# Seven block products in place of eight: the second output projection of a two-layer trunk

## The chip, the core and the metric

The kernel runs on one core of a Trainium2 chip. Its time is the device time of one execution in microseconds (us). It is written in a language in which the program gives each engine its instructions by name, and a planner sets the order on each engine's queue from priorities (program order) and its own estimate of durations. The engines are TensorE (PE; its weight loads are the row PEld), VectorE (DVE), ScalarE (ACT), GpSimd (POOL) and SyncE (SP), which here only starts DMAs.

## The reference

The input is one sequence of 1024 tokens of width 1024. Layer 0 is a differential attention, layer 1 a latent attention (MLA); both end in an output projection and a gated residual, and a last RMSNorm closes the trunk. What matters here is the end of layer 1:

```python
o = _from_blocks(lax.map(block, (_to_blocks(q_nope), _to_blocks(q_pe))))
o = o.reshape(b, s, MLA_WIDTH) * jax.nn.silu(z)
return o @ w_out                      # (1024 x 1024) @ (1024 x 1024)
...
x = x + gate * y                      # gate: one value per column
return _rmsnorm(x, final_norm_g)
```

## The kernel before

**Numbers in two parts.** Each float32 matrix operand is split into a high part, rounded to the format float32r (an ACT copy), and a low part, the rest (a subtraction on POOL or DVE). `mm3` (L184) multiplies high by high, high by low and low by high: three matmuls (L185, L186, L187) for one block of 128 rows by 512 columns.

**The second attention** (`attn1`, L1711) goes head by head; a head is eight row tiles of 128 queries. A tile is scores (L1704), softmax, transposes (L383), casts to high and low (L385 on ACT, L386 on DVE) and the product with the values (`pv`). Between them `fill` puts steps of the next head's projections into TensorE's gaps (`stream1`); their weight strips are split by L230 (ACT) and L231 (POOL). After each tile `extra` runs; in heads 0 to 6 it takes one step of `gate_steps` (56 steps), which computes the residual gate of layer 1 on DVE and stores it to DRAM (`gateS[1]`).

A finished half head goes through `finish` (L879): its row factors make a round trip through DRAM (L408, L410), POOL scales the tile (L885), ACT and POOL split it (L890, L891), and both parts are stored to DRAM (`oS`, L892, L893). `in_turn` keeps a POOL operation in program order, `behind` puts an operation behind a named one; the planner may move the rest.

**The second output projection** (`out_proj`, L1126) runs two groups of four token tiles, each over two column halves. For each of these four parts, all eight heads' weight blocks are loaded (L1088) and split (L1104 on ACT, L1105 on POOL), and four PSUM banks take 8 heads x 4 tiles x 3 matmuls. Then `resid` multiplies a bank by the gate, which is broadcast over the partitions (`oy`, L1152, DVE), and adds it to the residual tile (L1153). `done1` (L1826) takes the sum of squares (L1829, ACT), multiplies the first column half by the final gain on POOL (L1836) and, after the second half, computes the inverse root in seven small DVE operations (`rsqrt8k`, L178 to L181), scales both halves (L1843 on DVE, L1850 on ACT) and stores them. Two tiles, one tile, and one tile in two column pieces make the last part (`LAST`).

The last head (7) has no fills. There `extra1` loads the first group's attention output and the first weight blocks, and `PRE1` places five preparing steps, each one head of two tiles of the projection. Head 7's second half does not go through DRAM: `tail1` scales it by a product with a matrix of ones (L904), after a few projection matmuls.

Of the kernel before, what the change touches and what calls it, by code (L numbers as in the profile page):

```python
# [21 lines left out]
P = 128  # L22
# [24 lines left out]
V1_AT = (3, 2)  # L47
OT1_AT = 5
NORM_AT = 4
PRE0 = (0, 0, 0, 0, 0, 0, 1, 1, 1, 2, 1)  # L50
PRE1 = (0,0,0,0,0,0,1,1,1,1,1)
OW0 = (3, 4)
OP0 = (6, 4)
OW1 = (2, 4)
OP1 = (12, 4)
LAST = [(((0, 1, 2, 3), 0, HF),), (((0, 1), 0, HF), ((2,), 0, HF), ((3,), 0, 256), ((3,), 256, HF))]
Z_LAST = 4
# [9 lines left out]
X_ACT0 = (0, 2)  # L67
X_CUT = 256
WARM = (8, 9)
SIN_AT = (4, 5, 7)  # L70
# [16 lines left out]
def trunk(ctx: ExitStack, tc: tile.TileContext, A, out):  # L87
# [48 lines left out]
    vS = [[dr.tile([4, 2, P, 2, 4, P], F32, name=f"vS{l}_{f}") for f in range(2)] for l in range(2)]  # L136
    oS = [dr.tile([NH, 2, 2, P, HF], F32, name=f"oS{l}") for l in range(2)]
    x1S = dr.tile([NT, P, D], F32, name="x1S")
# [44 lines left out]

    def mm3(psum, ah, al, bh, bl, first, last):  # L184
        PE.matmul(psum, ah, bh, start=first, stop=False)  # L185
        PE.matmul(psum, ah, bl, start=False, stop=False)  # L186
        mm3.last = PE.matmul(psum, al, bh, start=False, stop=last).ins  # L187

# [690 lines left out]
    def finish(o, y, l, h, half, dst, ap_, dgs):  # L879

        if dst is None:
            b, rb = bcast_rows(ap_, y, "osq", 4)

            def scale():
                in_turn(G.tensor_mul(t3(o), t3(o), rb))  # L885
                hooks.append(split)

            def split():
                with behind("S"):
                    S.copy(b.bitcast(F32R), o)  # L890
                in_turn(G.tensor_sub(o.bitcast(F32R), o, b))  # L891
                SP.dma_start(oS[l][h, half, 0], b)  # L892
                SP.dma_start(oS[l][h, half, 1], o)  # L893
# [6 lines left out]
        rb = bank("m", "rb")  # L900
# [4 lines left out]
        V.tensor_mul(o, o, rb)  # L905
        hi, lo = dst
        S.copy(hi, o)
        V.tensor_sub(lo, o, f32v(hi))
# [217 lines left out]
    def out_proj(OT, ow, W0, pre, wpool, xpool, nlate, nx, xsrc, tile_done, group_done):  # L1126
# [4 lines left out]
        for gi in range(2):  # L1131
# [5 lines left out]
            for f in range(2):  # L1137
# [7 lines left out]
                for h in range(NH):  # L1145
                    W.append(W0[h] if first and h < len(W0) else ow.load(f, h))
                last = gi == 1 and f == 1

                def resid(i, a=0, b=HF, acc=None):
                    y = wpool.tile([P, HF], F32, name="oy", tag="oy", bufs=2)  # L1150
                    cs = slice(f * HF + a, f * HF + b)
                    V.tensor_mul(y[:, a:b], (acc or accs[i])[:, a:b], ow.gb[:, cs])  # L1152
                    add = V.tensor_add(fulls[i][:, cs], fulls[i][:, cs], y[:, a:b])  # L1153
                    tile_done(gi * 4 + i, fulls[i], cs.start, cs.stop, add)

                if last:
                    for tiles, a, b in LAST[ow.l]:
                        part = None
                        if a:
                            part = bank("acc", "oaccb")  # L1160
                        for h in range(NH):
                            for i in tiles:
                                mm_o(part or accs[i], OT, W, h, gi, i, slice(a, b))
                            if h % 2 or len(tiles) == 4:
                                side.tick()
                        for i in tiles:
                            resid(i, a, b, part)
                else:
                    for h in range(NH):
                        for i in range(2 if first and h < pre.n else 0, 4):  # L1170
                            mm_o(accs[i], OT, W, h, gi, i)
                        side.tick()
                    for i in range(4):
                        resid(i)
            group_done(gi, fulls)
# [10 lines left out]
    def extra0(i):  # L1186
# [3 lines left out]
        if i == Z_LAST:  # L1190
# [12 lines left out]
            ow = OutW(0, pw, *OW0)  # L1203
            ot = [lambda h=h: load_ot(OT[h][0], [oS[0][h, 0, i] for i in range(2)]) for h in range(NH - 1)]
            todo.extend(pre_plan(ot, ow, OW0[0], W0))
# [27 lines left out]
    mk.clear()  # L1233
    load_ot(OT[NH - 1][0], [oS[0][NH - 1, 0, i] for i in range(2)])
    st2b.close()
# [16 lines left out]

    def done0(tt, full, a, b, add):
        if b < D:
            return
# [24 lines left out]

    ot = [lambda h=h: load_ot(OT[h][1], [oS[0][h, 1, i] for i in range(2)]) for h in range(NH - 1)]
    side.add(None, None, *ot[:3], tail0, *ot[3:])
# [327 lines left out]
    def gate_steps():  # L1610
# [12 lines left out]
        for j in range(KT):  # L1623
# [9 lines left out]
        SP.dma_start(gateS[1].rearrange("(p j) -> p j", p=P), gcol1)  # L1633

    gate1 = gate_steps()


# [129 lines left out]
    stv.close()  # L1767
    ap2 = pool(st5, "attn1b")
    for h in range(NH - 1):
# [4 lines left out]
    assert next(gate1, 0) == 0  # L1774
    stw.close()
    stC.close()
    stO = ExitStack()
    op = pool(stO, "OT1", side="right")

    OT1 = [[pair(op, f"o1a{h}"), pair(op, f"o1b{h}") if h == NH - 1 else None] for h in range(NH)]  # L1780
    o7 = [op.tile([P, HF], F32, name="o17"), op.tile([P, HF], F32, name="dg17")]
    pw = pool(stO, "pw1", side="right")
    ow = OutW(1, pw, *OW1)
    W0 = []
    pre1 = Pre(OT1, W0)
    ot = [lambda h=h: load_ot(OT1[h][0], [oS[1][h, 0, i] for i in range(2)]) for h in range(NH - 1)]
    todo = pre_plan(ot, ow, OW1[0], W0)

    def extra1(i):
        for _ in range(-(-len(todo) // max(1, 7 - i))):  # L1790
            todo.pop(0)()
        for _ in range(PRE1[i]):
            pre1.step()

    def late1(o_, zz, gz):
# [3 lines left out]
        def f():  # L1799
            V.reciprocal(zz, zz)  # L1800
            finish(o, zz, 1, NH - 1, 1, OT1[NH - 1][1], None, dgs)

        return f

    tail1 = attn1(NH - 1, lambda i: (0, 0, 0, 0), extra1, late1)
    mk.clear()
    load_ot(OT1[NH - 1][0], [oS[1][NH - 1, 0, i] for i in range(2)])
    st5.close()
# [3 lines left out]

    psum("ps6", accx=5, m=1)
    st6 = ExitStack()
    p6 = pool(st6, "p6")
    for h in range(NH - 1):
        OT1[h][1] = pair(p6, f"o1b{h}")
    side.add(None, None, tail1, *[None] * OT1_AT, *[lambda h=h: load_ot(OT1[h][1], [oS[1][h, 1, i] for i in range(2)]) for h in range(NH - 1)])
    fg = p6.tile([P, D], F32, name="fg")
# [3 lines left out]
    held = []  # L1823
    w_ = [p6.tile([P, 1], F32, name=f"tw{tt}") for tt in range(NT)]

    def done1(tt, full, a, b, add):  # L1826
        ss = sm.tile([P, 1], F32, name="tss")
        junk = p6.tile([P, HF], BF16, name="tjunk", tag="tjunk", bufs=1)
        S.activation(junk[:, : b - a], full[:, a:b], AF.Square, accum_out=ss)  # L1829
        if tt == NT - 1 and b == D:  # L1830
            with tc.issue_after(add.ins):
                held.pop()()
        w = w_[tt]
        if a == 0:
            V.tensor_scalar(w, ss, 1.0 / D, EPS, op0=ALU.mult, op1=ALU.add)
            G.tensor_mul(full[:, a:b], full[:, a:b], fg[:, a:b])  # L1836
        else:
            V.scalar_tensor_tensor(out=w, in0=ss, scalar=1.0 / D, in1=w, op0=ALU.mult, op1=ALU.add)
        if b == D:
            y = rsqrt8k(w)[:, 0:1]  # L1840

            def second():
                V.scalar_tensor_tensor(out=full[:, HF:], in0=full[:, HF:], scalar=y, in1=fg[:, HF:], op0=ALU.mult, op1=ALU.mult)  # L1843
                SP.dma_start(out[tt][:, HF:], full[:, HF:])

            if tt == NT - 2:
                held.append(second)
            else:
                second()
            S.mul(full[:, :HF], full[:, :HF], y)  # L1850
            SP.dma_start(out[tt][:, :HF], full[:, :HF])

    out_proj(OT1, ow, W0, pre1, p6, p6, *OP1, [x1S[tt] for tt in range(NT)], done1, lambda gi, fulls: None)
    st6.close()
# [81 lines left out]
```

## Time and profile before

| what | value |
|---|---|
| median of 3 runs | 1436.45 us (1434.03 to 1439.59) |
| the profiled execution | 1437.65 us, of which the span of instructions is 1435.9 us |
| granted TensorE clock, mean | 0.996 |
| DMA | 213.18 MB, mean 148 GB/s |
| weight blocks of both output projections (`wor`) | 64 loads of 256 KB |
| second attention, head 7 | about 1290 to 1344 us |
| second output projection | first preparing step at 1326, last matmul at 1427 |

In the profile a busy TensorE is not TensorE at its peak, because its matmuls overlap: a 128x512 matmul of the projection has a duration of some 390 ns while the next one starts much earlier. So distances between starts are read, not durations. For the other engines durations can be added up. "Idle before" names what an engine waited for last.

### The profile page before, as it was taken

To read this page: it belongs to the slowest core of one execution; us is meant where nothing else is said; L and a number is where in the kernel's file an instruction comes from. 1 tells how busy PE (TensorE), PEld (TensorE's weight loads), DVE (VectorE), ACT (ScalarE), POOL (GpSimd) and SP (SyncE) were. 2 spreads that over 40 slices of the span, in tenths; PEclk is the share of its full clock that TensorE was granted. 3 is DMA by queue.
4 is the path that set the end of the run, shared out by engine and by line. 5 is a ranking of instruction groups with operands and counts; after the bars stand their busy time and mean duration, and the time that the engine had idled before them with its cause. 6 is when DMAs were issued, how large, how long until landed. Compare 5 with 4: busy or idle time off the path is not lost. (4 is left out here: it accounts for less than half of the span.)

```text
span 1435.9 us, 20702 instructions
## 1 busy us (share of the span) xinstructions
PE 1398.5 (97%) x7426; PEld 1165.9 (81%) x7426; DVE 921.5 (64%) x1377; ACT 727.2 (51%) x1287; POOL 612.9 (43%) x485
## 2 busy tenths in 40 slices
PE   9999999999999999998999999999999999999997
PEld 6777788888888887887787877887888888888886
DVE  8655777777777767677345985545666555555356
ACT  5523465656565655566343442345454454545342
POOL 5425264646464655454552234531141331412572
PEclk9999999999999999999999999999999999999999
DMA  9776533334342324237653146398343433336563
GB/s 343 244 242 204 185 89 107 82 110 118 103 111 85 104 77 112 58 96 263 230 175 125 37 133 205 123 299 242 112 135 106 135 105 82 97 102 205 185 237 135
DMA packets 135385, 213.18 MB, mean 148 GB/s; under 512 B 19057, under 2 KB 56049, under 8 KB 135282
## 3 DMA queue, kind: packets, MB, share of 16 engines
q1 hardware_dynamic: 135282, 211.86, 47.8%
q8 instruction: 58, 0.95, 0.3%
q14 instruction: 45, 0.37, 0.1%
HBM read 137.40 MB, written 50.80 MB: 131 GB/s over the span
## 5 line engine op out<-in xcount | busy, mean ns | idle before, releaser
L385 ACT CAST pth<-tr 128x512 fp32r<-128x512 f32 x256 | 150.3, 587 | 284.9 <-PE tr L383 283.1
L400 DVE TENSOR_REDUCE nm<-s 128x1 f32<-128x1024 f32 x192 | 233.9, 1218 | 69.9 <-PE s L847 58.4
L386 DVE TENSOR_TENSOR ptl<-tr,pth 128x512 fp32r<-128x512 f32 x256 | 176.0, 688 | 140.3 <-ACT pth L385 140.0
L231 POOL TENSOR_TENSOR wl<-wraw,wh 128x512 fp32r<-128x512 f32 (+2 forms) x79 | 105.1, 1333 | 205.1 <-ACT wh L230 170.1
L402 ACT ACTIVATE e<-s,nm 128x1024 f32<-128x1024 f32 x128 | 143.6, 1122 | 30.8 <-DVE nm L400 28.4
L383 PE MATMUL tr<-ident,e 128*128 128x128 f32 x1024 | 155.0, 274 | 2.5 <-DVE ptl L386 2.4
L383 PEld LDWEIGHTS tr<-ident,e 128*128 128x128 f32 x1024 | 121.1, 140 | 43.6 <-DVE ptl L386 19.4
L185 PE MATMUL acc<-h0h,wh 128*128 128x512 f32 x360 | 150.1, 417 | 1.0 <-DVE v_hl L363 1.0
L185 PE MATMUL pv<-pth,vt 128*128 128x256 f32 x512 | 147.6, 288 | 0.9 <-DMA vt<-vS 0.9
L186 PE MATMUL pv<-ptl,vt 128*128 128x256 f32 x512 | 145.7, 284 | 0.0
L187 PE MATMUL pv<-pth,vt 128*128 128x256 f32 x512 | 144.7, 283 | 0.0
L187 PE MATMUL acc<-h0h,wl 128*128 128x512 f32 x360 | 143.2, 398 | 0.6 <-POOL wl L231 0.6
L186 PE MATMUL acc<-h0l,wh 128*128 128x512 f32 x360 | 142.0, 394 | 0.0
L1105 POOL TENSOR_TENSOR wol<-wor,woh 128x512 fp32r<-128x512 f32 x64 | 85.5, 1358 | 84.9 <-ACT woh L1104 84.3
L185 PEld LDWEIGHTS pv<-pth,vt 128*128 128x128 f32 x512 | 97.4, 190 | 4.3 <-issue 1.1
L186 PEld LDWEIGHTS pv<-ptl,vt 128*128 128x128 f32 x512 | 97.6, 191 | 2.7
L187 PEld LDWEIGHTS pv<-pth,vt 128*128 128x128 f32 x512 | 97.6, 191 | 0.0
L847 PE MATMUL s<-ks,qa 128*128 128x512 f32 x256 | 82.6, 404 | 6.1 <-DVE e L855 4.4
L327 POOL TENSOR_TENSOR rp_r<-rp_raw,cosT 128x512 f32<-128x512 f32 x38 | 50.0, 1316 | 85.6 <-ACT rp_raw L324 38.6
L332 POOL TENSOR_TENSOR rp_sw<-rp_sw,sinT 128x512 f32<-128x512 f32 x42 | 55.2, 1314 | 73.2 <-DMA rp_sw<-rp_raw 73.1
L855 DVE SCALAR_TENSOR_TENSOR e<-s,z,e 128x1024 f32<-128x1024 f32 x64 | 82.1, 1283 | 2.1
L187 PEld LDWEIGHTS acc<-h0h,wl 128*128 128x128 f32 x360 | 67.6, 188 | 16.3 <-POOL wl L231 1.0
(599 smaller groups left out, 3370.9 us busy)
## 6 DMA issues: line engine op xcount, KB each, us to landing
ada<-in_ada_ss SPq DMA_DIRECT2D x32, 512.0 KB, 5.6
wraw<-in_w_s SPq DMA_DIRECT2D x64, 256.0 KB, 2.9
vS<-v_hl SPq DMA_DIRECT2D x32, 512.0 KB, 5.9
vt<-vS SPq DMA_DIRECT2D x32, 512.0 KB, 3.9
wor<-in_w_out SPq DMA_DIRECT2D x64, 256.0 KB, 3.6
rp_sw<-rp_raw SPq DMA_DIRECT2D x168, 64.0 KB, 2.0
bc_s<-bc_d SPq DMA_DIRECT2D x34, 256.0 KB, 4.2
oS<-bc_s SPq DMA_DIRECT2D x30, 256.0 KB, 2.4
```

The costliest lines, as they stand in the source:

```text
L185: PE.matmul(psum, ah, bh, start=first, stop=False)
L186: PE.matmul(psum, ah, bl, start=False, stop=False)
L187: mm3.last = PE.matmul(psum, al, bh, start=False, stop=last).ins
L231: sub = (V if pair_of else G).tensor_sub(l_[:, :n], raw[:, :n], f32v(h_[:, :n]))
L383: PE.transpose(tr[:, j, :], p[:, kt * P : (kt + 1) * P], ident)
L385: mk["S"] = S.copy(pth[kh][:, :, dst], tr).ins
L386: mk["V"] = V.tensor_sub(ptl[kh][:, :, dst], tr, f32v(pth[kh][:, :, dst])).ins
L400: mk["V"] = V.reduce_max(nm, s_ps, axis=AX.X, negate=True).ins
L402: mk["S"] = S.activation(e, s_ps, AF.Exp, bias=nm, scale=1.0, accum_out=zs).ins
L847: PE.matmul(s_ps[:, kc * HF : (kc + 1) * HF], src[:, c, ql], KS[h][kc][:, c, :], start=fst, stop=not fst)
L855: combined.append(V.scalar_tensor_tensor(out=e0, in0=e1, scalar=z1[:, 0:1], in1=e0, op0=ALU.mult, op1=ALU.add).ins)
L1105: in_turn(G.tensor_sub(lo, raw, f32v(hi)))
```

## The change

The 1024 x 1024 product is cut into 2 x 2 blocks of 512: A11 and A12 are the heads 0 to 3 and 4 to 7 of the first 512 tokens, A21 and A22 those of the second 512; B11 to B22 are the blocks of the output weights, already multiplied by the gate. Seven products and sums (Winograd's form of Strassen's scheme, which the kernel also uses for its gate path) take the place of eight:

| n | left operand | right operand | goes to (token half, column half) |
|---|---|---|---|
| 0 | A11 | B11 | all four |
| 1 | A12 | B21 | first, first |
| 2 | A21 + A22 - A11 | B22 - B12 + B11 | the other three |
| 3 | A21 + A22 | B12 - B11 | both halves of the second columns |
| 4 | A12 minus the left operand of 2 | B22 | first, second |
| 5 | A11 - A21 | B22 - B12 | second, both |
| 6 | A22 | B21 minus the right operand of 2 | second, first |

- `gate_steps` goes on after the gate is stored: in 28 more of its steps (28 to 55, from head 3's second half) it loads the gate and, head by head of four, the four weight blocks, multiplies them by the gate and forms the seven right operands on POOL, and stores them to DRAM (`tS`).
- The attention's output is stored whole (`oF`), not split. `pair_steps` forms the left operands of 2 to 5 on POOL: pairs 0 and 1 (heads 0 and 4, 1 and 5) in head 6, stored to DRAM (`sS`); pair 2 in head 7, kept in SBUF; pair 3 is formed by DVE in `tail1`.
- Before each product its blocks are fetched, and split by `split_a` (ACT and DVE; ACT and POOL in head 7) and `split_w` (ACT and POOL). PSUM banks Y hold products 0 + 2 + 5 + 6, banks Z first product 1 and then 3 + 4. Each time a bank is right for a quarter of the output, one DVE add puts it on the residual.
- In products 0 to 2 the head is the outer loop, in 3 to 5 the token tile. Tokens 0 to 511 are finished after product 4, with the inverse root on POOL; tokens 512 to 1023 after product 6, whose tiles go as before (`LAST1`).
- `PRE1` places four preparing steps of product 0 instead of five. `out_proj` loses its case for the last part; layer 0's work is the same.

```diff
+    oF = dr.tile([NH, 2, P, HF], F32, name="oF")
+    tS = dr.tile([7, 4, P, HF], F32, name="tS")
+    sS = dr.tile([4, 2, P, HF], F32, name="sS")
...
             def split():
+                if l == 1:
+                    SP.dma_start(oF[h, half], o)
+                    return
...
         SP.dma_start(gateS[1].rearrange("(p j) -> p j", p=P), gcol1)
+        yield
+        gb = [ut("gb", True, F32) for _ in range(2)]
+        for f in range(2):
+            SP.dma_start(gb[f], gateS[1][None, f * HF : f * HF + HF].to_broadcast([P, HF]))
+        for h in range(4):
+            (b11, b12), (b21, b22) = b_ = [[ap3.tile([P, HF], F32, name="ob", tag="ob", bufs=nob) for _ in range(2)] for _ in range(2)]
+            for m in range(2):
+                for f in range(2):
+                    SP.dma_start(b_[m][f], A["w_out1"][f, 4 * m + h])
+            yield
+            for f in range(2):
+                for m in range(2):
+                    in_turn(G.tensor_mul(b_[m][f], b_[m][f], gb[f]))
+            yield
+            for n, t in ((0, b11), (1, b21), (4, b22)):
+                SP.dma_start(tS[n, h], t)
+            t2 = ap3.tile([P, HF], F32, name="ot2", tag="ob", bufs=nob)
+            in_turn(G.tensor_sub(b12, b12, b11))
+            in_turn(G.tensor_sub(t2, b22, b12))
+            yield
...
+        yield from pair_steps(0)
+        yield
+        yield from pair_steps(1)
+
+    def pair_steps(h):
...
+        for t, (hh, half) in zip(a, ((h, 0), (h + 4, 0), (h, 1), (h + 4, 1))):
+            SP.dma_start(t, oF[hh, half])
+        yield
+        in_turn(G.tensor_add(a22, a21, a22))
+        in_turn(G.tensor_sub(a21, a11, a21))
+        in_turn(G.tensor_sub(a11, a22, a11))
+        in_turn(G.tensor_sub(a12, a12, a11))
...
+        def put(self, raw, hi, lo, eng):
+            with behind("S"):
+                S.copy(hi, raw)
+            sub = eng.tensor_sub(lo, raw, f32v(hi))
...
+    def add_to(tt, acc, f, a=0, b=HF, piece=False):
+        full = xs_[tt]
+        cs = slice(f * HF + a, f * HF + b)
+        add = V.tensor_add(full[:, cs], full[:, cs], acc[:, a:b])
...
+    for h in range(4):
+        for i in range(4):
+            sv.mm(2, Y[i], h, i)
+        if h == 1:
+            sv.fetch(4)
+            load_x1(1, 1)
+    for i in range(4):
+        add_to(i, Y[i], 1)
+
+    Z = [bank("z", "oz") for _ in range(4)]
+    for n, first, rows, acc, f, piece in ((3, True, 4, Z, 1, False), (4, False, 0, Z, 1, True), (5, False, 4, Y, 1, True)):
+        sv.split(n + 1)
+        for i in range(4):
+            for h in range(4):
+                sv.mm(n, acc[i], h, i, start=first)
...
+            add_to(rows + i, acc[i], f, piece=piece)
+            if i == 1 and n < 5:
+                sv.fetch(n + 2)
...
+    for tiles, a, b in LAST1:
+        acc = {i: bank("z", "oyb") if a else Y[i] for i in tiles}
+        for h in range(4):
+            for i in tiles:
+                sv.mm(6, acc[i], h, i, slice(a, b), start=a > 0)
+        for i in tiles:
+            add_to(4 + i, acc[i], 0, a, b, piece=True)
```

More of the change, by code (lines that the diff above doesn't have):

```diff
@@ L68 @@
 X_CUT = 256
+PAIR_AT = 4
 WARM = (8, 9)
@@ L1146, in out_proj @@
                     W.append(W0[h] if first and h < len(W0) else ow.load(f, h))
-                last = gi == 1 and f == 1
-                def resid(i, a=0, b=HF, acc=None):
-                    y = wpool.tile([P, HF], F32, name="oy", tag="oy", bufs=2)
[L1151 to L1174, printed above, removed]
+                for h in range(NH):
+                    for i in range(2 if first and h < pre.n else 0, 4):
+                        mm_o(accs[i], OT, W, h, gi, i)
+                    side.tick()
+                for i in range(4):
+                    y = wpool.tile([P, HF], F32, name="oy", tag="oy", bufs=2)
+                    V.tensor_mul(y, accs[i], ow.gb[:, fs])
+                    V.tensor_add(fulls[i][:, fs], fulls[i][:, fs], y)
+                    if f:
+                        tile_done(gi * 4 + i, fulls[i])
             group_done(gi, fulls)
@@ new lines, in trunk, with step, home_w @@
+    class Pre7:
+        n = 0
+        def step(self):
+            if not self.n:
+                self.accs = [bank("acc", "oy") for _ in range(2)]
+            for i in range(2):
+                sv.mm(0, self.accs[i], self.n, i, start=True)
+            self.n += 1
+    pw = pool(stO, "pw1", side="right")
+    sv = Seven()
+    sv.raw = lambda: pw.tile([P, HF], F32, name="wor", tag="wor", bufs=4)
+    def home_w(n, h):
+        pl, tag, nb = (pw, "wo", 8) if h < 2 else (p6, "wp", 8) if n else (wst, "whl", 6)
+        return [pl.tile([P, HF], F32R, name="wo" + x_, tag=tag, bufs=nb) for x_ in "hl"]
@@ L1789, in extra1 @@
+    todo += [lambda h=h: sv.fetch_a(2, h) for h in range(2)]
     def extra1(i):
+        if PAIR_AT <= i < 8:
+            next(pair2, None)
         for _ in range(-(-len(todo) // max(1, 7 - i))):
```

216 lines of the change are left out of this document (171 added, 45 removed).

## The prediction

> **What bounds the kernel now.** I read the page's engine table first, then the stretches from the middle of the second attention to the end, then the waits of TensorE there, then the timeline of the last 22 us. The engine table:
>
> ```profile
> PE 1398.5 (97%) x7426; PEld 1165.9 (81%) x7426; DVE 921.5 (64%) x1377; ACT 727.2 (51%) x1287; POOL 612.9 (43%) x485
> ```
>
> The stretches (columns: stretch, length, then busy us and count of PE, PEld, DVE, ACT, POOL, the granted clock, DMA share, GB/s) are: heads 3 to 6 of the second attention, head 7, the projection up to the two last-but-one tiles, and the end.
>
> ```profile
> 1130.00:1290.00 160.00, 160.00 (x972) 137.49 (x971) 86.82 (x119) 82.41 (x151) 49.28 (x39) 1.00 0.34 96
> 1290.00:1344.00 54.00, 54.00 (x348) 47.25 (x347) 28.69 (x42) 29.53 (x53) 15.89 (x13) 1.00 0.55 173
> 1344.00:1416.00 72.00, 71.30 (x314) 57.97 (x314) 34.31 (x72) 26.01 (x53) 45.82 (x33) 1.00 0.66 230
> 1416.00:1435.90 19.90, 11.58 (x74) 10.31 (x72) 14.63 (x47) 6.09 (x14) 3.04 (x3) 0.85 0.28 106
> ```
>
> TensorE is filled without a hole from 1130 to 1416, at the full granted clock. Busy alone could deceive, since matmuls overlap; the waits of TensorE from 1344 to the end settle it. There are two entries in all:
>
> ```profile
> PE oacc L186 <- POOL wol L1105: 0.7, 1, 0.7
> PEld oacc L186 <- POOL wol L1105: 1.1, 1, 1.1
> ```
>
> So until 1416 matmuls taken away shorten the run, as long as nothing else becomes late. The pace of one matmul comes from the stretch that holds only projection matmuls (its columns are PE, PEld, DVE):
>
> ```profile
> 1348.96:1413.80 64.84, 64.84 (x281) 52.85 (x282) 8.20 (x12) 1.00 0.68 239
> ```
>
> 64.84 / 281 = **0.231 us** for one 128x512 matmul, start to start.
>
> The last 20 us are another case. The timeline (start, duration, engine, line), TensorE first, then VectorE:
>
> ```profile
> 1415.94 0.40 PE L187 MATMUL oacc<-woh,o1b7l 128*128 128x512 f32 x1
> ...
> 1421.48 0.40 PE L187 MATMUL oacc<-woh,o1b7l 128*128 128x512 f32 x1
> ...
> 1427.30 0.28 PE L187 MATMUL oaccb<-woh,o1b7l 128*128 128x256 f32 x1
> ```
>
> ```profile
> 1415.67 1.40 DVE L1152 TENSOR_TENSOR oy<-oacc,gb 128x512 f32<-128x512 f32 x2 [0.96 <-PE oacc L187]
> 1416.99 2.60 DVE L1153 TENSOR_TENSOR xfull<-xfull,oy 128x512 f32<-128x512 f32 x2
> ...
> 1423.66 0.68 DVE L1152 TENSOR_TENSOR oy<-oacc,gb 128x512 f32<-128x512 f32 x1
> 1424.38 0.69 DVE L1153 TENSOR_TENSOR xfull<-xfull,oy 128x512 f32<-128x512 f32 x1
> ...
> 1428.21 0.42 DVE L1152 TENSOR_TENSOR oy<-oaccb,gb 128x256 f32<-128x256 f32 x1
> 1428.66 0.42 DVE L1153 TENSOR_TENSOR xfull<-xfull,oy 128x256 f32<-128x256 f32 x1
> ```
>
> Tiles 4 and 5 of the last group are ready at 1415.7 to 1416.3. Tile 6 is ready near 1421.9, but VectorE takes it at 1423.66, 1.8 us late; the last piece is ready near 1427.6 and taken at 1428.21. From 1415.7 on VectorE sets the pace: 20.2 us to the end of the span.
>
> **The change, part by part.** All terms are against the profiled execution (1437.65 us, of which 1435.9 are its span). It stands 1.2 us above the median of 1436.45, so a difference is carried over to the median unchanged.
>
> *Matmuls.* Before there are 2 token groups x 2 column halves x 8 heads x 4 tiles x 3 = 384. After there are 7 products x 4 x 4 x 3 = 336. The 48 fewer would be 48 x 0.231 = 11.1 us if TensorE set the end. It does so only up to the point where tiles 4 and 5 of the last part are ready, and the change takes 24 from each side of that point: before it, 384 - 48 = 336 become 336 - 24 = 312. **First term: 24 x 0.231 = -5.5 us.** The wait for L1105 above need not come again: -0.5 (bounds 0 and -1.1).
>
> *The end.* After, one add from PSUM stands where L1152 and L1153 stood, because the gate is now in the weights. If VectorE keeps its order and its lag, the stretch from the two tiles to tile 6's turn was 8.0 us (1415.67 to 1423.66), holding 4.0 of L1152 and L1153; two adds from PSUM at 0.69 leave 5.4. From there to the last piece was 4.55; without its L1152 pieces (0.68 + 0.42) it is 3.45. From the last add to the end of the span 1435.9 - 1428.66 = 7.2. Together 16.1, so -4.1. If VectorE keeps up with TensorE, the last piece is ready 24 x 0.231 = 5.5 us after the two tiles (before it was 11.6), and the end is 5.5 + 0.1 + 7.2 = 12.8 later, so -7.4. Tile 6 and the last tile now come twice as fast, so VectorE's lag is likelier than not to stay: **second term -5.2 us** (bounds -4.1 and -7.4).
>
> *Feeding the products.* A product is 48 matmuls, 11.1 us. For each, four weight blocks and four activation blocks are split: eight ACT casts, four POOL subtractions, four DVE subtractions. From 1344 to the end the groups are:
>
> ```profile
> L1104 ACT CAST woh<-wor 128x512 fp32r<-128x512 f32 x24 | 14.7, 617 | 32.3 <-DMA wor<-in_w_out 22.8 <-PE oacc L186 5.1 <-PE oacc L187 2.3
> L1105 POOL TENSOR_TENSOR wol<-wor,woh 128x512 fp32r<-128x512 f32 x26 | 35.6, 1392 | 24.9 <-ACT woh L1104 24.3 <-DMA wor<-in_w_out 0.3
> L1836 POOL TENSOR_TENSOR xfull<-xfull,fg 128x512 f32<-128x512 f32 x8 | 11.9, 1520 | 0.0
> L1153 DVE TENSOR_TENSOR xfull<-xfull,oy 128x512 f32<-128x512 f32 x15 | 18.4, 1252 | 0.0
> L1152 DVE TENSOR_TENSOR oy<-oacc,gb 128x512 f32<-128x512 f32 x15 | 10.3, 688 | 24.3 <-PE oacc L187 24.3
> ```
>
> Per product: ACT 8 x 0.62 = 4.9; POOL 4 x 1.39 = 5.6; DVE 4 x 0.69 to 1.25 for the subtractions plus 4 x 0.69 for the adds = 5.5 to 7.8. All lie under 11.1. The tight place is products 4, 5 and 6: from product 3 on the row tile is the outer loop, so the previous product's weight blocks come free only at its end. The next but one can be split from there on and is due 11.1 us later; ACT then POOL need 0.6 + 5.6 = 6.2. That leaves 5 us for the L1836 products and the final scaling that share these engines. The gate path of this layer is the near relative: it runs seven products per pair of heads, with one weight split per 12 matmuls, the same rate. In its whole stretch (880 to 990) its products waited for a split only here:
>
> ```profile
> PEld zacc L187 <- POOL wl L231: 1.5, 2, 1.1
> PE zacc L187 <- POOL wl L231: 0.7, 1, 0.7
> ```
>
> Its three pairs are 21 splits, so TensorE's own wait is 0.03 us a split, and 24 splits here would make 0.8. I take **+0.5 us** (bounds 0 and +4, the L1836 products all ahead of the splits once: 11.7 + 0.6 against 11.1 in each of three products).
>
> VectorE with two SBUF operands slows beside POOL: the pair at 1416.99 above takes 1.3 each while POOL works on L1836, and 0.69 at 1424.38 when POOL rests; L1152 with one PSUM operand stays at 0.69. [...]
>
> *Weights made during the attention.* From step 28 of the gate steps (head 3, tile 4) to the end of head 6, POOL gets 32 + 8 operations more and loses seven L891; ACT loses seven casts (L890). SP gets 62 more DMAs (18 loads of weights and gate, 28 stores of products, 8 loads and 8 stores of sums; 256 KB each) and loses 7 stores (L892, L893 become one). The rows for 1130 to 1290:
>
> ```profile
> L891 POOL TENSOR_TENSOR o<-o,bc_s 128x512 fp32r<-128x512 f32 x7 | 9.0, 1291 | 25.3 <-ACT bc_s L890 25.3
> L231 POOL TENSOR_TENSOR wl<-wraw,wh 128x256 fp32r<-128x256 f32 x3 | 2.2, 736 | 16.7 <-ACT wh L230 16.7
> SPq L408 <- DVE zz L1723: 49.5, 7, 9.3
> SPq L1715 <- DVE o L1722: 16.4, 5, 10.5
> wraw<-in_w_kn SPq DMA_DIRECT2D x2, 128.0 KB, 2.3
> vt<-vS SPq DMA_DIRECT2D x6, 512.0 KB, 3.4
> ```
>
> POOL rises from 49.3 to 49.3 + 40 x 1.29 - 9.0 = 92 us of 160, DMA traffic from 96 GB/s by (62 - 7) x 0.26 MB / 160 us = 90 to 186 GB/s, about head 7's level, where TensorE did not wait either. What counts is order: POOL's operations here are kept in program order, so a burst of four multiplications (5.2 us) stands ahead of a strip's lower half (L231). The timeline of TensorE in head 5 shows the beat, two tiles from score to score and the fills (acc) between:
>
> ```profile
> 1212.45 0.39 PE L187 MATMUL acc<-ckh,wl 128*128 128x512 f32 x1
> ...
> 1216.08 0.63 PE L1704 MATMUL s<-kn_h,qn_h 128*128 128x512 f32 x2
> ...
> 1219.29 0.39 PE L187 MATMUL acc<-ckh,wl 128*128 128x512 f32 x1
> ...
> 1220.42 0.40 PE L187 MATMUL acc<-ckh,wl 128*128 128x512 f32 x1
> ...
> 1223.87 0.40 PE L187 MATMUL acc<-ckh,wl 128*128 128x512 f32 x1
> ...
> 1227.42 0.63 PE L1704 MATMUL s<-kn_h,qn_h 128*128 128x512 f32 x2
> ```
>
> Two tiles are 11.3 us, so a gate step is 5.7. A strip is needed two fill steps after its split; the fills come 6.8, 1.1 and 3.5 us apart, so two steps are 4.6 to 10.4 us, and after the cast and the subtraction about 3 us remain in the worst case. A full burst would then cost 5.2 - 3 = 2.2 us; with four weight bursts and two of sums the worst is 13 us, nothing at all is the other end. Most split points have the longer distance: I take **+1 us**.
>
> *Head 7.* POOL goes from 5 weight splits and one L891 to 17 operations (15.9 + 14 = 30 of 54 us), ACT from 5 casts to 13 (29.5 + 5 = 34.5 of 54). A cast put ahead of a transposed tile's cast delays TensorE by at most 0.62; 8 more would be 5 us, none 0. ACT mostly waits for TensorE there, so **+0.5 us**. One preparing step fewer (4, not 5) is only moved, and counted in the 336. The loads (18 blocks against 19) stay.
>
> Sum: -5.5 - 0.5 - 5.2 + 0.5 + 1 + 0.5 = **-9.2 us**: 1428.4 for the profiled execution, 1427.2 on the median, say **1427 us**.
>
> **The rivals.**
> - *The strips come late* (0.18). The POOL bursts hit half of the time at full price: +6.5 in place of +1, so -3.7: 1433. For it: strict order on POOL. Against: 68 us of room in 160.
> - *The splits come late at products 4 to 6* (0.10). POOL's 5.6 plus four L1836 (6.1) are 11.7 against 11.1, and ACT's final scaling is queued between; at most +4 in place of +0.5, so -5.7: 1431. Against: the gate path's 0.03 us a split.
> - *SP makes POOL stand* (0.14), the slower side. The weight loads of a round are issued one step (5.7 us) before POOL needs them and land 3 us after issue. SP already stands for up to 9.3 and 10.5 us behind one semaphore (rows above). If such a wait lies ahead of the loads, POOL stands for 9.3 + 3 - 5.7 = 6.6 us with the strip behind it, which costs 6.6 - 3 = 3.6 us, and the later blocks of the round follow. Over six rounds that is 22 us: 1427 - 1 + 22 = 1448. It decides once SP is more than 5.7 us late; below that it costs nothing. Against: a load that waits for nothing can be issued ahead of a waiting one when the order is planned.
> - That the matmuls do not become fewer cannot be: 336 follows from the loops.
>
> **How the numbers follow.** The forecast has 0.58: its own range is 1422 (all good ends: -5.5 - 1.1 - 7.4 = -14) to 1431. The late strips at 1433 and late splits at 1431 lie inside a range of **1422 to 1436**, which leaves out the slower rival (0.14) and some 0.03 of the strips' worst end (+13: 1439). About 0.5% (7.2 us, so 1429.3) is what a measurement of this kernel can tell from no change: faster is the forecast's 0.58 and half of the late splits, 0.63; same is the strips and the other half, 0.23; slower 0.14.
>
> **What would show it.** Right: TensorE still free of waits between products; about 67.5 us from the attention's last matmul to the point where the last part's first two tiles are ready (72 before, with 18 more matmuls in it); 13 to 16 us from there to the end; heads 3 to 6 as long as before. Wrong: TensorE waiting for POOL's strips in heads 4 to 6, PEld waiting for a weight block at the start of products 4 to 6, POOL idle with a DMA as the releaser during the weight rounds, or ACT casts ahead of the transposed tiles in head 7.

## The result: no difference, and the profile after

| what | before | after |
|---|---|---|
| median | 1439.51 us (22 runs, 1434.03 to 1445.95) | 1439.81 us (22 runs, 1432.23 to 1444.01) |
| ratio after / before | | 1.000, 95% interval 0.9987 to 1.0013 |
| profiled execution, its span | 1437.65, 1435.9 us | 1440.16, 1438.4 us |

The forecast was 1427 us, with 1422 to 1436 as its range. It was wrong: seven products take as long as eight. The engine table of the profile after, then its stretches (heads 3 to 6 of the second attention, head 7, the products up to the last part's first two tiles, the end; columns as in the prediction):

```profile
PE 1391.9 (97%) x7366; PEld 1159.4 (81%) x7366; DVE 934.3 (65%) x1368; ACT 729.8 (51%) x1295; POOL 660.2 (46%) x526
```

```profile
1132.30:1292.30 160.00, 160.00 (x972) 137.50 (x971) 87.41 (x119) 78.92 (x144) 91.66 (x72) 1.00 0.57 179
1292.30:1349.20 56.90, 54.12 (x341) 46.94 (x340) 30.61 (x45) 33.33 (x61) 24.60 (x19) 0.97 0.46 134
1349.20:1423.80 74.60, 69.59 (x298) 55.49 (x297) 50.79 (x65) 31.68 (x65) 53.06 (x40) 0.98 0.56 194
1423.80:1438.40 14.60, 6.21 (x39) 5.42 (x37) 10.26 (x42) 5.86 (x14) 0.00 (x0) 0.88 0.37 144
```

TensorE is busy for 7 us less, yet it now has holes in head 7 (54.12 of 56.90) and between the products (69.59 of 74.60), and in both the granted clock falls below 1.00. VectorE rises from 34.3 to 50.8 us in the third stretch. What TensorE waited for from 1350 to the end (us in all, times, longest) was VectorE's add L1969, never a weight block:

```profile
PE oy L186 <- DVE x L1969: 3.8, 2, 3.2
PE oz L186 <- DVE x L1969: 1.2, 2, 0.6
```

To compare parts, I measure between the same operations in both traces: VectorE's gating of a half head (L1722 before, L1760 after), the start of the attention's last pv matmul, the add for tile 4 in the last part (before: L1152), the end of the span.

| from, to | before | after | difference | prediction |
|---|---|---|---|---|
| the first half of head 0, the first half of head 7 | 1008.19 to 1323.79 = 315.6 | 1010.48 to 1326.26 = 315.8 | +0.2 | +1 |
| the first half of head 7, last pv | to 1343.70 = 19.9 | to 1349.17 = 22.9 | +3.0 | -0.9 |
| last pv, tile 4 of the last part | to 1415.67 = 72.0 | to 1423.76 = 74.6 | +2.6 | -4.2 |
| tile 4, the end | to 1435.9 = 20.2 | to 1438.4 = 14.6 | -5.6 | -5.2 |

In the prediction's column, 6 of the 24 matmuls fewer (the preparing step, 1.4 us) fall on head 7 and 18 (4.2 us) on the products. The four differences add up to +0.2. The other 2.3 us of the spans' difference arise before the first row, where every engine's instructions are the same; the variants below, which have these same instructions there, made that half of head 0 between 1004.7 and 1011.6 us, so it is chance between executions. Two parts came as predicted, and two lost what the others gained.

**Head 7.** ACT's timeline (start, duration, and in brackets the idle time before and its end):

```profile
1331.96 0.59 ACT L386 CAST pth<-tr 128x512 fp32r<-128x512 f32 x1
1336.07 0.62 ACT L1858 CAST oah<-wor 128x512 fp32r<-128x512 f32 x1 [3.52 <-DMA wor<-sS]
1336.60 1.11 ACT L403 ACTIVATE e<-s,nm 128x1024 f32<-128x1024 f32 x1
...
1337.70 0.57 ACT L386 CAST pth<-tr 128x512 fp32r<-128x512 f32 x1
1340.17 0.62 ACT L1858 CAST oah<-wor 128x512 fp32r<-128x512 f32 x1 [1.90 <-DMA wor<-sS]
```

The casts of product 2's left operands are written down after the attention, but the planner put them into ACT's queue ahead of the last softmax (L403) and of the transposed tiles' casts. In this trace ACT takes its queue in order: the softmax's input (nm, L401 on VectorE) was ready at 1332.7, but it stood behind a cast whose load SP had issued only at 1333.29. TensorE saw this two operations on, at the transposes, which wait for VectorE's L387:

```profile
1336.20 0.40 PE L188 MATMUL oy<-woh,oal 128*128 128x512 f32 x1
1339.38 1.11 PE L384 MATMUL tr<-ident,e 128*128 128x128 f32 x4 [2.78 <-DVE ptl L387]
...
1341.14 0.63 PE L188 MATMUL oy<-woh,oal 128*128 128x512 f32 x1
1341.57 0.63 PE L186 MATMUL oy<-woh,oah 128*128 128x512 f32 x1
```

After the pause the matmuls start 0.43 us apart instead of 0.23; the granted clock from 1339.38 to 1342.75 is 0.52. This slow clock did not make the head longer. In four variants below whose head 7 has the same casts in the same place (finish_later, splits_behind_adds, twelve_slots, weight_lows_by_act) TensorE kept its full rate, 0.23 us from start to start, paused twice, for 2.9 to 3.0 and 1.1 to 1.3 us, and the second row of the table is 22.8 to 23.1 us, as here. The casts' waits set the length.

**The products.** VectorE's timeline from the end of product 3 (products are numbered 0 to 6):

```profile
1388.72 1.27 DVE L1969 TENSOR_TENSOR x<-x,oz 128x512 f32<-128x512 f32 x2
1393.32 0.69 DVE L1859 TENSOR_TENSOR oal<-wor,oah 128x512 fp32r<-128x512 f32 x1 [3.33 <-ACT oah L1858]
...
1399.88 0.68 DVE L1969 TENSOR_TENSOR x<-x,oz 128x512 f32<-128x512 f32 x1
1401.40 0.16 DVE L1985 SCALAR_TENSOR_TENSOR tw<-tss,tw 128x1 f32<-128x1 f32 x1 [0.85 <-ACT tjunk L1975]
1402.58 0.75 DVE L1991 SCALAR_TENSOR_TENSOR x<-x,rq_y,fg 128x512 f32<-128x512 f32 x1 [1.02 <-POOL rq_y L2003]
1403.25 0.68 DVE L1969 TENSOR_TENSOR x<-x,oz 128x512 f32<-128x512 f32 x1
...
1415.41 0.68 DVE L1969 TENSOR_TENSOR x<-x,oy 128x512 f32<-128x512 f32 x1
```

At 1390.0 it reaches product 6's splits, which are queued ahead of product 3's last two adds, and stands for ACT, which stands for a load:

```profile
1392.67 0.62 ACT L1858 CAST oah<-wor 128x512 fp32r<-128x512 f32 x1 [9.01 <-DMA wor<-oF]
```

So product 4's first add comes at 1399.88, while TensorE had filled that bank by 1392.4 (the last of its 12 matmuls starts at 1392.15): a lag of 7.5 us. From there each tile of product 4 is finished in a chain: add, wait 0.85 for ACT's square, L1985, wait 1.0 for POOL's root, L1991. That is 1403.25 - 1399.88 = 3.4 us for each of the first two tiles, where TensorE makes one in 2.8 (12 x 0.231), so the lag isn't made up. The last two take 4.7 and 4.1 us; beside POOL's subtractions (1409.50 to 1413.73) L1991 takes 1.77 us in place of 0.75. Product 5's first add is done at 1416.1, and product 6 accumulates on the same banks:

```profile
1412.60 0.40 PE L188 MATMUL oy<-woh,oal 128*128 128x512 f32 x1
1416.24 0.47 PE L186 MATMUL oy<-woh,oah 128*128 128x512 f32 x1 [3.24 <-DVE x L1969]
...
1419.19 0.63 PE L186 MATMUL oy<-woh,oah 128*128 128x512 f32 x1
```

It can be worked out: from 1392.4 to product 6's turn at 1412.8 are 20.4 us; VectorE needs 1416.1 - 1399.9 = 16.2 from its first add. It may lag 4.2 us for nothing; it lagged 7.5, and TensorE waited 3.2. (The weight load's own entry for this wait, 3.7 us on PEld, names ACT's L1998, which was done at 1415.5; the load starts at 1416.20, right behind VectorE's add.)

### The profile page after: what moved, and what is told of

The parts are those of the page before. It is cut to its first block, busy times and chain, and to the rows that moved or that the text cites. A ratio compares the mean times of both kernels' runs of the same rounds, so it can differ in the third digit from the quotient of the medians.

```text
span 1438.4 us, 20700 instructions
## 1 busy us (share of the span) xinstructions
PE 1391.9 (97%) x7366; PEld 1159.4 (81%) x7366; DVE 934.3 (65%) x1368; ACT 729.8 (51%) x1295; POOL 660.2 (46%) x526
## 5 line engine op out<-in xcount | busy, mean ns | idle before, releaser
L401 DVE TENSOR_REDUCE nm<-s 128x1 f32<-128x1024 f32 x192 | 234.0, 1219 | 70.7 <-PE s L848 58.9
L387 DVE TENSOR_TENSOR ptl<-tr,pth 128x512 fp32r<-128x512 f32 x256 | 176.1, 688 | 136.5 <-ACT pth L386 136.0
L403 ACT ACTIVATE e<-s,nm 128x1024 f32<-128x1024 f32 x128 | 143.5, 1121 | 29.9 <-DVE nm L401 27.7
L328 POOL TENSOR_TENSOR rp_r<-rp_raw,cosT 128x512 f32<-128x512 f32 x38 | 49.9, 1314 | 90.1 <-ACT rp_raw L325 37.9
L848 PE MATMUL s<-ks,qb 128*128 128x512 f32 x256 | 80.6, 396 | 0.0
```

Of the source, the lines that this page charges most:

```text
L387: mk["V"] = V.tensor_sub(ptl[kh][:, :, dst], tr, f32v(pth[kh][:, :, dst])).ins
L401: mk["V"] = V.reduce_max(nm, s_ps, axis=AX.X, negate=True).ins
L403: mk["S"] = S.activation(e, s_ps, AF.Exp, bias=nm, scale=1.0, accum_out=zs).ins
L848: PE.matmul(s_ps[:, kc * HF : (kc + 1) * HF], src[:, c, ql], KS[h][kc][:, c, :], start=fst, stop=not fst)
```

## The experiments

Ratios are to the kernel before, run anew beside each group of variants; "us less" is what the ratio makes of that kernel's median (1437.7 to 1438.1 us), with an interval of some 2 to 3 us on either side. Lines below an edit can shift by some 10. "Distances" are the table's second and third rows, 22.9 and 74.6 us in the changed kernel.

**casts_behind**

```diff
-    mk.clear()
+    last_pth = mk.pop("S"); mk.clear()
...
-    sv.split(2)
+    with tc.issue_after(last_pth): sv.split(2)
```

> The ACT casts of product 2's left operands (L1858, oah<-wor) are put behind the attention's last cast of a transposed tile; nothing else moves. Measured by the distance from the store of head 7's first half (L891) to the attention's last pv matmul: 19.9 us before the change (1323.8 to 1343.7), 22.9 after it (1326.3 to 1349.2). Theory (ACT stands for the DMA of wor in front of exp and pth, and TensorE's clock drops after the pause): distance 19.5 to 20.5, TensorE's 2.8 us wait for DVE gone, time 3 to 4 us under the changed kernel, ratio to the kernel before 0.997 to 0.998. Rival 1 (the softmax shows because one preparing step is missing at tile 6): distance 22 to 23, ratio 1.000. Rival 2 (the head ends earlier, but the products then wait for their loads): distance near 20, ratio 1.000, a new DMA wait at products 0 to 2.

(The times named there, 1323.8 and 1326.3, are those of VectorE's gating of the half, not of its store.) Measured: 1433.2 us, ratio 0.9971 (0.9957 to 0.9984), 4.2 us less. Distances 19.2 (1323.72 to 1342.90) and 73.4. TensorE's longest wait in the head's last tiles, and the softmax on ACT:

```profile
1334.61 0.66 PE L384 MATMUL tr<-ident,e 128*128 128x128 f32 x4 [0.57 <-DVE ptl L387]
```

```profile
1330.27 1.11 ACT L403 ACTIVATE e<-s,nm 128x1024 f32<-128x1024 f32 x1 [0.26 <-DVE nm L401]
```

The theory holds: the wait of 2.8 is 0.57, and the products still had their own 3.2 us wait. The edit holds back all of product 2's splits; by the two traces what it moved out of the head's last tiles are three ACT casts and the three VectorE subtractions (L1859) that read them.

**step_at_tile_6**

```diff
-PRE1 = (0, 0, 0, 0, 0, 0, 0, 1, 1, 1, 1)
+PRE1 = (0, 0, 0, 0, 0, 0, 1, 1, 1, 1, 0)
```

> PRE1 gets a preparing step at tile 6 again and none at the last place (four steps as in the changed kernel); the casts stay ahead in ACT's queue. The distance from the store of head 7's first half to the last pv matmul now holds one step of 1.4 us more behind which work can hide. Theory (ACT stands for DMA): the casts still stand, 3.5 and 1.9 us, the step fills at most 1.4 us of TensorE's pause: ratio 0.999. Rival (missing step): the pause goes, ratio 0.997.

Measured: 1439.87 us, ratio 1.0011 (0.9996 to 1.0025). Distances 24.7 and 74.9. (Both kernels have the same four steps, 24 matmuls, ahead of the last pv; the step is only earlier.) The casts still stood, one of them longer:

```profile
1330.54 0.62 ACT L1858 CAST oah<-wor 128x512 fp32r<-128x512 f32 x1 [4.22 <-DMA wor<-sS]
```

TensorE's pause grew to 4.2 us, and the head took 1.8 us longer; the theory's own 0.999 lies outside the interval too. The rival is out: a step at tile 6 does not help while a cast waits for a load at the head of the queue.

**finish_later**

```diff
+        later.append([])
+        with tc.issue_after(add.ins):
+            for fn in later.pop(0):
+                fn()
...
-            V.scalar_tensor_tensor(out=w, in0=ss, scalar=1.0 / D, in1=w, op0=ALU.mult, op1=ALU.add)
...
+            later[0].append(root)
+            later[1].append(scale)
```

Here `root` makes tw and the root, and comes behind the next add; `scale` makes L1991 and the stores, behind the one after.

> The finishing of product 4's tiles is put off on VectorE: a tile's tw comes behind the next tile's add, its scaling (L1991) behind the one after; product 5's tw likewise. Same operations, other order. Theory (VectorE stands for ACT's square, 0.85 us, and POOL's root, 1.0 us, in each tile, so product 5's adds, which product 6 needs, come late): TensorE's waits for L1969 at product 6 (3.2 and 0.6 us) and the slow clock behind them (1.4 us) go, time 4 to 5.5 us under the changed kernel, ratio 0.996 to 0.997. Rival (VectorE is late by its amount of work, slowed beside POOL, and not by standing): the waits shrink by 1 us at most, ratio 0.999 to 1.000.

Measured: 1432.9 us, ratio 0.9957 (0.9937 to 0.9976), 6.2 us less; second distance 68.0. TensorE's waits from 1345 on are a single one, at product 4:

```profile
PE oz L186 <- DVE x L1969: 0.9, 1, 0.9
```

VectorE did the same work, still stood for the late loads (product 4's first add lags 6.4 us, at 1394.84), and the waits at product 6 were gone. So the chain is a necessary part of the loss.

**all_three**: the two edits and a third, which puts product 6's splits behind product 3's last add.

```diff
-        sv.split(n + 1)
+        with tc.issue_after(add3[-1]) if n == 5 else nullcontext(): sv.split(n + 1)
...
+            add3 = add3 + [add_to.last] if n == 3 else add3
```

> The casts behind, the finishing put off, and product 6's splits behind product 3's last add on ACT and VectorE (they stood 9.0 us for wor<-oF ahead of two adds). Theory: the losses are apart in time and add up, -3.5 - 5 - 1 to 1.5: time 1429 to 1431 where the kernel before has 1439.5, ratio 0.993 to 0.995. Rival (one loss only hides another: TensorE, no longer late, waits for the loads or splits of products 5 and 6): ratio 0.997 or more, with PEld waiting for L1858 or L1859.

Measured: 1428.03 us where the kernel before had 1437.66, ratio **0.9926** (0.9905 to 0.9948): 10.6 us less, the best of the study. The last two stretches and TensorE's only wait from 1335 to the end:

```profile
1340.30:1408.00 67.70, 67.03 (x297) 54.63 (x296) 50.53 (x64) 30.65 (x65) 50.64 (x39) 1.00 0.62 214
1408.00:1423.00 15.00, 6.28 (x39) 5.43 (x38) 10.71 (x43) 6.51 (x16) 2.04 (x2) 0.81 0.36 140
```

```profile
PE oz L186 <- DVE x L1969: 0.7, 1, 0.7
```

The gains add up within their intervals (4.2 + 6.2 = 10.4), and the distances, 67.7 and 15.0 us, are those of the prediction: about 67.5 and 13 to 16 us. The third edit shows no gain of its own that these intervals could tell.

**splits_behind_adds**: the changed kernel with only product 6's left splits moved, behind product 4's last add.

```diff
-                self.split_a(n, h)
+                with tc.issue_after(after) if after else nullcontext(): self.split_a(n, h)
...
-        sv.split(n + 1)
+        sv.split(n + 1, add_to.last if n == 5 else None)
```

> Product 6's splits of its left operands (ACT casts and L1859 on VectorE, which stood for wor<-oF until 1393 to 1397 ahead of product 3's last two adds and all of product 4's) are put behind product 4's last add. The finishing of a tile stays as it is: add, wait for ACT's square, tw, wait for POOL's root, L1991, 3.4 us per tile. Theory (the late loads start the lag, and the chain of 3.4 us against TensorE's 2.8 only keeps it): product 4's first add comes at once, near 3 us after the product's start and not 10, product 5's adds are done before product 6, TensorE's waits of 3.2 and 0.6 us go: ratio 0.996 to 0.997. Rival (the chain makes the lag by itself): TensorE waits 2 us or more for L1969 at product 6: ratio 0.999.

Measured: 1436.47 us, ratio 0.9988 (0.9976 to 1.0), which is the rival's number. But the profile shows that the edit had not done what it was for. VectorE made product 4's first add at once (1391.66), then ACT:

```profile
1391.94 0.62 ACT L1858 CAST oah<-wor 128x512 fp32r<-128x512 f32 x1 [9.44 <-DMA wor<-oF]
1392.46 2.18 ACT L1858 CAST woh<-wor 128x512 fp32r<-128x512 f32 x4
1394.55 0.62 ACT L1976 ACTIVATE tjunk<-x 128x512 bf16<-128x512 f32 x1
```

The cast still stood for the load, now ahead of the square that VectorE waited for; the root then stood behind POOL's four lower halves, and the first tile's scaling (L1992 here) came at 1399.10. Counted from the last pv that is 50.9 us, where it was 53.4. The late load had for the most part only found another queue, so this run does not decide between the two.

**twelve_slots**

```diff
-    sv.raw = lambda: p6.tile([P, HF], F32, name="wor", tag="wor", bufs=8)
+    sv.raw = lambda: p6.tile([P, HF], F32, name="wor", tag="wor", bufs=12)
```

> The changed kernel with 12 slots for raw blocks (wor) in the last part where it has 8; SP's order is the same, VectorE's but for one pair. The loads of product 6 (wor<-oF) no longer wait for POOL to free a slot. Theory (VectorE's lag comes from these late loads and is kept by the chain of 3.4 us per tile): wor<-oF lands before 1388, ACT does not stand 9.0 us for it, product 4's first add comes within 3 us of its bank, TensorE's waits for L1969 at product 6 (3.2 and 0.6 us) fall under 1 us, ratio 0.996 to 0.997. Rival (VectorE is late at 1390 anyway, because its subtractions take 1.8 us beside POOL): waits of 2 us or more remain, ratio 0.999 to 1.000.

Measured: 1433.55 us, ratio 0.9969 (0.9954 to 0.9983), 4.5 us less; second distance 68.7 (1350.15 to 1418.86). ACT's wait for the load, counted from the attention's last matmul, ends at 37.0 us (43.5 in the changed kernel), and TensorE's waits from 1350 on:

```profile
1387.10 0.62 ACT L1858 CAST oah<-wor 128x512 fp32r<-128x512 f32 x1 [3.80 <-DMA wor<-oF]
```

```profile
PE oz L186 <- DVE x L1969: 0.6, 1, 0.6
PE oy L186 <- DVE x L1969: 0.6, 1, 0.6
```

This is the clean test. The chain is as it was (1399.19 to 1402.55, 3.4 us for the first tile), but product 4's first add now lags some 3 us (1396.28 for a bank filled by 1393.4), under the 4.2 that are free. The load was late because SP waited for a slot that POOL had yet to empty: SP's waits for POOL's L1859 are 8.5 us between 1378 and 1395 in the changed kernel, and it issues product 6's first block of the attention's output 37.9 us after the last pv there and 31.2 us after it here (first line: changed kernel):

```profile
1387.04 0.38 SPq L1833 DMA_DIRECT2D wor<-oF  x1
```

```profile
1381.36 0.38 SPq L1833 DMA_DIRECT2D wor<-oF  x1
```

**weight_lows_by_act**

```diff
-            self.put(raw, hi, lo, G)
+            if n > 1: S.copy(hi, raw); S.copy(lo, raw)
+            else: self.put(raw, hi, lo, G)
```

> For products 2 to 6 the weight blocks' low parts are not computed: ACT copies the block into them in place of POOL's subtraction. TensorE's work is the same; POOL is free but for fg, the L1983 products and the roots, ACT has 20 more copies of 0.62 us. If VectorE's subtractions with two SBUF operands are slow because POOL works beside them: L1859 on VectorE takes 0.69 where it took 1.2 to 1.8, VectorE has holes between 1354 and 1390, and the raw blocks come free earlier, so wor<-oF lands before VectorE needs it. Theory of the late loads: then the waits at product 6 go, ratio 0.996 to 0.997. Theory of the chain alone: they stay at 2 us or more, ratio 0.999. If the slowdown has another cause, L1859 stays at 1.2 to 1.8.

Measured: 1430.14 us, ratio 0.9944 (0.9929 to 0.9958); second distance 66.8, no wait of TensorE between products. The same two groups of VectorE's splits from 1350 to 1400 (count, then busy time, mean ns of one, and idle before), first in the changed kernel, then here:

```profile
L1859 DVE TENSOR_TENSOR oal<-oa,oah 128x512 fp32r<-128x512 f32 x3 | 5.3, 1781 | 0.0
L1859 DVE TENSOR_TENSOR oal<-o1k,oah 128x512 fp32r<-128x512 f32 x3 | 4.3, 1417 | 0.0
```

```profile
L1860 DVE TENSOR_TENSOR oal<-o1k,oah 128x512 fp32r<-128x512 f32 x3 | 2.1, 688 | 0.0
L1860 DVE TENSOR_TENSOR oal<-oa,oah 128x512 fp32r<-128x512 f32 x3 | 2.1, 686 | 0.9 <-ACT oah L1859 0.9
```

POOL's neighbourhood costs VectorE up to 1.1 us a split. The chain stays at 3.4 us (1395.32 to 1398.69) and TensorE does not wait, so the chain alone is not enough either. The run changes two things at once: VectorE's splits are faster, and the slots come free earlier (ACT casts the first wor<-oF 35.6 us after the last pv). It does not say what each is worth.

**weights_8_columns**

```diff
-                    in_turn(G.tensor_mul(b_[m][f], b_[m][f], gb[f]))
+                    in_turn(G.tensor_mul(b_[m][f][:, :8], b_[m][f][:, :8], gb[f][:, :8]))
...
```

The four subtractions are cut to 8 columns in the same way.

> In the second attention POOL makes only 8 of 512 columns of each of the seven right operands (the rest of the products, and of the sums, is left out); same DMAs, same order on POOL up to tile names, 32 operations of some 1.3 us become very short. If the bursts delay the projections' strips, heads 3 to 6 become shorter by up to 6 us (ratio 0.996); if they hide, as the equal distances of 315.6 and 315.7 us between the same two tiles of head 2 and head 7 before and after say, the ratio stays within 0.001 of 1.000.

Measured: 1437.98 us, ratio 1.0007 (0.9995 to 1.0019). The distance in the table's first row (from head 0, which the expectation calls head 2) is 315.7 (1007.98 to 1323.68). POOL's multiplications in heads 3 to 6, in the changed kernel and here:

```profile
L1633 POOL TENSOR_TENSOR ob<-ob,gb 128x512 f32<-128x512 f32 x16 | 20.2, 1300 | 0.0
```

```profile
L1633 POOL TENSOR_TENSOR ob<-ob,gb 128x8 f32<-128x8 f32 x16 | 2.7, 203 | 0.0
```

POOL's work on the weights is hidden, as far as this interval can tell.

**casts_later_splits** and **casts_later_slots** are variants of all_three. In place of its third edit, the first has the edit of splits_behind_adds and the second has the twelve slots.

> The casts of product 2 behind the attention, the finishing put off, and product 6's left operands split behind product 4's last add (all_three with the third edit moved further back). Theory: nothing stands ahead of product 4's adds now, TensorE has no wait over 1 us from the attention's end to the last part; ratio 0.992 to 0.993, the same as all_three, since the late loads cost nothing once the finishing is put off. Rival: the late loads cost something of their own, 1 to 2 us: 0.991 to 0.992.

> casts_behind and finish_later together, with 12 slots and product 6's splits where the planner puts them. Theory: each loss is cured already, so the slots bring nothing more than 1 us: ratio 0.992 to 0.993, as all_three. Rival (TensorE still loses time to late accumulators at products 3 to 5): 0.990 to 0.991.

Measured: 1429.4 us, ratio 0.9945 (0.9926 to 0.9963), and 1428.43 us, ratio 0.9936 (0.9915 to 0.9956). The intervals overlap with that of all_three: once the finishing is put off, earlier or later loads make no difference that shows here.

## Why the prediction was wrong, step by step

Two terms of the sum failed: the feeding of the products, put at +0.5 us, took 6.9 in the trace, and head 7, put at +0.5, took 4.4. The others came out near their size.

- **The matmuls (-5.5) and the wait on L1105 (-0.5)** were right. With both losses cured, the second distance is 67.7, within 0.2 us of the prediction's. No run showed TensorE waiting for a weight block's lower half.
- **The end (-5.2)** was right in size, -5.6, but in part by luck. The sum had 8.9 us from the two tiles to the last add if VectorE's lag stayed and 5.6 if it went, and 7.2 from there on. Measured are 6.5 and 8.1 (in the lines below tile 6's add and the last one, 1430.27 against 1423.76 and 1438.4). VectorE took tile 6 some 0.9 us late where it was 1.8, so the lag was more than half gone; the last stretch grew by 0.9, with tile 6's small operations now mixed with the last tile's.

```profile
1428.05 0.68 DVE L1969 TENSOR_TENSOR x<-x,oy 128x512 f32<-128x512 f32 x1
...
1430.27 0.41 DVE L1969 TENSOR_TENSOR x<-x,oyb 128x256 f32<-128x256 f32 x1
```

- **Weights made during the attention (+1)** was within its bounds, nearer to zero: +0.2, and taking the work away gains nothing. The rival of late strips (0.18) did not happen, nor did SP make POOL stand at a price. Some 8.0 us of POOL's idle time in heads 3 to 6 ended with a load of the sums (oa<-oF in the row of the strips' lower halves below), and the half heads came in the same rhythm.

```profile
L232 POOL TENSOR_TENSOR wl<-wraw,wh 128x384 fp32r<-128x384 f32 (+1 forms) x8 | 7.7, 966 | 25.0 <-ACT wh L231 12.3 <-DMA oa<-oF 8.0 <-issue 4.7
```

- **Head 7 (+0.5, bounds 0 and +5)** was mis-sized, with the mechanism half seen. The prediction named an ACT cast ahead of a transposed tile's cast and priced it at the cast's own 0.62 us. What it did not ask is whether the cast's input is there when its turn comes: ACT took its queue in order here, and the price of the cast was its wait, 3.5 and 1.9 us. Against the prediction's starting point (19.9 less the six matmuls, 18.5) the head took 4.4 us more; casts_behind gave back 3.7 of it.
- **Feeding the products (+0.5, bounds 0 and +4)** failed. Its place, "products 4, 5 and 6", was right, and its object was wrong. It counted engines' work per product against 11.1 us and looked for late weight blocks. The weight blocks came in time. What came late were the accumulators, which VectorE must add up before product 6 may go on in the same banks. Two things met: loads that waited for a raw slot, so that VectorE entered product 4 with a lag of 7.5 us, and a chain of waits for ACT and POOL in each tile that was slower than TensorE. twelve_slots took away most of the first, finish_later the second, and each alone was worth 4.5 to 6.2 us. In the trace the stage cost 74.6 - 67.7 = 6.9 us, beyond the bound of +4, because busy time (VectorE 50.8 of 74.6) says nothing of such a chain.
- **VectorE beside POOL** was seen in the trace of the kernel before, and the prediction counted 0.69 to 1.25 us for each of VectorE's splits. The direction is confirmed, the size was too small: in the changed kernel a split takes 0.69 us with POOL idle (1393.32, 1394.61) and 1.78 beside POOL's subtractions (1368.69, 1370.39). That it is one of the reasons for VectorE's lateness fits the trace, since VectorE had no hole over 0.8 us from 1354.5 to 1390, but no run shows it by itself.

Of the 10.6 us that all_three gains, the prediction's -9.2 had the right parts; the two terms of half a microsecond each were the ones that decided.

## What to carry to other kernels

Ask of every operation that a planner may move forward in an engine's queue what it waits for, not only how long it takes: here ACT's cast of 0.62 us held up what was queued behind it for the 3.5 us that it stood for its load, and an ordering edge to the last urgent operation (casts_behind) gained 4.2 us. Where a product accumulates in a bank that another engine must first read, follow the reader's chain per tile, round trips included, and compare it with TensorE's time per tile: with 3.4 us against 2.8 here, a lag of 7.5 us at the first tile of product 4 was 8.1 at the second (1403.25 for a bank filled by 1395.15). Before judging that a saving "went nowhere", cut the run at the same operations in both traces: here the end gained 5.6 us, and head 7 and the products lost it.

## What the runs showed of the hardware

**Two engines in step.** While POOL and VectorE both subtracted with two SBUF operands, VectorE's splits started 1.70 to 1.71 us apart, and POOL did nine in 15.39 us, 1.71 each:

```profile
1368.69 1.78 DVE L1859 TENSOR_TENSOR oal<-oa,oah 128x512 fp32r<-128x512 f32 x1
1370.39 1.78 DVE L1859 TENSOR_TENSOR oal<-dg,oah 128x512 fp32r<-128x512 f32 x1
```

```profile
1357.94 15.39 POOL L1859 TENSOR_TENSOR wol<-wor,woh 128x512 fp32r<-128x512 f32 x9
```

With POOL idle (1387.65 to 1395.17 in the changed kernel) VectorE's next operation starts 0.60 us after a split (1388.12 to 1388.72, 1394.61 to 1395.21); the split's own duration is 0.69, so VectorE's durations, too, add up to more than its time. POOL took 1.28 us for each of seven such subtractions in the kernel before, while VectorE was busy for 2.29 of their 8.97 us:

```profile
1373.63 8.97 POOL L1105 TENSOR_TENSOR wol<-wor,woh 128x512 fp32r<-128x512 f32 x7 [1.89 <-ACT woh L1104]
```

Beside each other the two are slower, VectorE's by 1.1 us and POOL's by 0.4; the pair's 1.71 is some 0.2 less than the two one after the other, 0.60 + 1.28 = 1.88. How the one holds up the other no run here shows.

**The clock after a pause.** After its pause of 2.8 us in head 7 TensorE ran at 0.43 us a matmul for some 3 us, six matmuls at about 0.2 us more each. After the 3.2 us at product 6 three matmuls came at the full rate; behind a further wait of 0.6 us, eight came at 0.43 (granted clock 0.53 from 1417.70 to 1421.30). In finish_later it waited 3.0 and 1.3 us in head 7, and the granted clock (the last column but two) stayed at 1.00. The stretches that hold the matmuls behind the first pause, in the changed kernel and in finish_later:

```profile
1340.00:1345.00 5.00, 5.00 (x21) 3.95 (x20) 2.59 (x4) 2.21 (x4) 0.00 (x0) 0.74 0.00 0
```

```profile
1335.00:1340.00 5.00, 3.68 (x19) 2.88 (x20) 2.15 (x5) 2.21 (x4) 0.00 (x0) 1.00 0.09 33
```

So pauses of like length were followed by different clocks: 2.8 us by 0.52 in one trace, 3.0 us by 1.00 in another. What decides between them no run here shows.
